# Split products of a two-block transformer: three 256-column matmuls per weight tile become a 512-column one and a 256-column one

## The chip, the core and the metric

The program runs on one core of a Trainium2 chip. The metric is the device time of one execution in microseconds. Lower is better. Operands and result are in device memory, and all work between them is timed.

## What is computed

Two residual blocks of depth 2 work on 256 tokens of width 1024. The first (A) has an adaptive modulation, a mix of dilated attention, a recurrent state scan and spatial gating, and a gated feed-forward net with a short convolution. The second (B) has two gated feed-forward nets around a mix of attention and a depthwise convolution, and a gated projection. Cut to the parts that carry the large products:

```python
def first_block(...):
    for l in range(DEPTH):
        h = modulate(rms_norm(x, norm_mix[l]), sh1, sc1)
        p = h @ w_in[l]
        ...
        branch = jnp.einsum('bsnw,nwd->bsnd', ys, w_branch[l])
        merged = jnp.sum(gates * branch, axis=2)
        x = x + gt1[:, None, :] * (merged @ w_out[l])
        h = modulate(rms_norm(x, norm_ffn[l]), sh2, sc2)
        x = x + gt2[:, None, :] * conv_gated_ffn(h, ffn_w_up[l], ...)

def conv_gated_ffn(h, w_up, conv_w, conv_b, w_down):
    up = h @ w_up
    ...
    return (jax.nn.gelu(a) * g) @ w_down
```

All operands are float32.

## The kernel before, in words

Activations lie with features on the partitions and the 256 tokens along the free dimension (S = 256). A large product runs over tiles of 128 output features by 128 input features, here called k-tiles. Since TensorE takes the operands in a rounded form (fp32r), each operand is cut in two: a rounded large part (`hi` of a weight, `h` of an activation) and the rest (`lo`, `l`). A k-tile is then three matmuls that add up in one PSUM bank (`mm3`, L163 to L166): hi with h, hi with l, lo with h, each with 256 columns. Each loads its 128x128 weights by itself.

Weights come from device memory in pieces of up to 1024 columns (`wload`, L122): a DMA to `raw` (L133, SyncE's queue), ScalarE rounds to `hi` (L137), VectorE subtracts to `lo` (L138). The buffers are rings (`ring`), so loads and splits run ahead of the matmuls by a few pieces. Activations are split by `split` (L194; ScalarE L201, VectorE L202).

`fpair` (L168) fills one bank of 512 columns with two output tiles. Four banks (tag `mm`) go round for this. The bank is then read by whatever the stage does with it: VectorE multiplies by a row of norm factors (L993 in `ffn_b`, L1189 and L1195 in `mix_b`), or merges (L867 and L868 in `branch`), or ScalarE applies a function. `down` (L927) fills half a bank with an output tile of 22 k-tiles. `tpair` (L182) is the product with tokens on the partitions.

The stages run one after the other: `mix_a`, `ffn_a` for each layer, then `ffn_b`, `mix_b`, `ffn_b`, `pe_b` for each layer. In the mixes, chains of dependent small steps (attention, state scan, convolution) are put between the large products in program order by `Order`. In `mix_b` the convolution's last 24 taps of 4 tiles run on VectorE (L1183), while TensorE computes gates. Within an engine, instructions run in program order, which the build has already rearranged: a split of weights stands ahead of the reads of earlier banks.

The lines around the change are these:

```python
        mm(ps, w[0], x[0], start=first, stop=False)
        mm(ps, w[0], x[1], start=False, stop=False)
        mm(ps, w[1], x[0], start=False, stop=last)
```

Of the kernel before, what the change touches and what calls it, by code (L numbers as in the profile page):

```python
# [17 lines left out]
S = 256  # L18
# [32 lines left out]
class K:  # L51
    def __init__(self, tc, ctx, ins):
# [4 lines left out]
        self.hp = E(tc.tile_pool(name="hp", bufs=17))  # L57
# [59 lines left out]
    def ring(self, kind):  # L117
        """The next slot of the weight buffers; further pools take part in turn."""
# [65 lines left out]
    def tpair(self, w, x, tt):  # L184
        ps = self.ps()
        mm = self.nc.tensor.matmul
        sl = slice(tt * 128, tt * 128 + 128)
        for k in range(8):
            h, l = w(k * 256, 256)
            mm(ps[:, :256], x[k][0][:, sl], h, start=k == 0, stop=False)  # L190
            mm(ps[:, :256], x[k][1][:, sl], h, start=False, stop=False)  # L191
            mm(ps[:, :256], x[k][0][:, sl], l, start=False, stop=k == 7)  # L192
# [38 lines left out]
    def rms(self, x, spread=True, tail=False, both=False):  # L231
        """1/rms of the tokens on all partitions: in PSUM, or in SBUF with spread; with both also tokens on partitions."""
# [22 lines left out]
    def headsum(self, sq, n, ps=None):  # L255
        """Sums of 64-row halves of the n [128, S] slices of sq, tokens on partitions: [128, n*2*2]."""
# [8 lines left out]
    def headback(self, r, i, ps):  # L265
        """Spreads column group i of r back over the rows of each half: [128, S] into ps."""
# [63 lines left out]
# ------------------------------------------------------------------ block A  # L330
# [11 lines left out]
class LayerA:  # L342
    """Per-layer columns and small weights of block A."""

    def __init__(self, G, l, pool, cact, first=None, late=None):
# [10 lines left out]
        else:  # L356
            # the columns of the first modulation before all else
# [26 lines left out]
def mod_cols(G, L, i, norm):  # L384
    """(A, shift) with h = x*rstd*A + shift."""
# [342 lines left out]
def mix_a(G, L, x, l, mp, pre, dbg=None):  # L728
# [841 lines left out]
```

## Time and profile before

| | |
|---|---|
| time, median of 3 runs | 2327.91 us (2326.52 to 2330.79) |
| span of the profiled execution | 2323.2 us |
| median less span | 4.7 us |
| busy TensorE matmul / weight load | 2240.6 / 2142.4 us |
| busy VectorE / ScalarE | 1677.5 / 1276.9 us |
| data moved | 416.69 MB, mean 179 GB/s |

The profiled execution has no time of its own beside its span, so the span is set against the median of the runs. Matmuls are pipelined and their ends are modelled, so TensorE's busy share says little of how fast it goes. What counts is the distance between the starts of two matmuls, or their number in a stretch.

### The profile page before, as it was taken

How to read it: one execution, taken by the hardware profiler on the slowest of the kernel's cores; microseconds unless marked ns; L12 is line 12 of the kernel's file. 1: busy time of each engine (PE TensorE's matmuls, PEld its weight loads, DVE VectorE, ACT ScalarE, POOL GpSimd, SP SyncE). 2: the span in 40 equal slices, each digit the busy share in tenths (PEclk: the TensorE clock that was granted, in tenths of full speed). 3: DMA queues.
4: the chain of work that ended last, by engine and by line, in shares of the span. 5: the costliest groups of instructions: out<-in, count | busy, mean ns of one | idle time of the engine just before them, and what ended most of it. 6: DMA issues, size and time to landing. Idle time of an engine off the chain costs nothing.

```text
span 2323.2 us, 46766 instructions
## 1 busy us (share of the span) xinstructions
PE 2240.6 (96%) x19122; PEld 2142.4 (92%) x19122; DVE 1677.5 (72%) x3026; ACT 1276.9 (55%) x2144; POOL 0.2 (0%) x4
## 2 busy tenths in 40 slices
PE   4999998978999999999999999999999999999999
PEld 4888898978888889999999999899999999999999
DVE  7777767757677776877576659976667655997665
ACT  4574545544457464565454457654455446666444
POOL 0000000000000000000000000000000000000000
PEclk9999999989999999999999999999999999999999
DMA  7634457777663445875576563466565556346653
GB/s 294 190 118 128 142 177 242 250 199 231 191 199 116 137 129 167 266 228 159 169 237 182 161 208 109 131 211 186 156 210 183 174 168 200 109 138 216 183 158 124
DMA packets 129117, 416.69 MB, mean 179 GB/s; under 512 B 14564, under 2 KB 20324, under 8 KB 128134
## 3 DMA queue, kind: packets, MB, share of 16 engines
q1 hardware_dynamic: 126718, 409.50, 55.8%
q10 hardware_dynamic: 2184, 4.19, 0.9%
q8 instruction: 150, 2.46, 0.4%
q14 instruction: 65, 0.53, 0.1%
HBM read 408.40 MB, written 5.24 MB: 178 GB/s over the span
## 4 chain that ended last, share of the span: by engine, by line
PE 80%; DMA 8%; DVE 7%; ACT 4%; issue 1%; SPq 0%; ACTq 0%; DVEq 0%
PE ps L164 23%; PE ps L165 22%; PE ps L166 22%; DMA raw<-in_ffn_up 3%; DVE lo L138 2%; DMA raw<-in_w_ada 2%; ACT hi L137 1%; DMA raw<-in_w_in 1%; PE rec L582 1%; PE rec L590 1%; DVE raw L369 1%; PE rec L1178 1%; DVE raw L338 1%; PE rec L636 1%; PE ps L191 1%
## 5 line engine op out<-in xcount | busy, mean ns | idle before, releaser
L164 PE MATMUL ps<-h,hi 128*128 128x256 f32 x5080 | 1438.4, 284 | 31.9 <-ACT h L201 29.6
L166 PE MATMUL ps<-h,lo 128*128 128x256 f32 x5080 | 1433.4, 283 | 14.7 <-DVE lo L138 14.7
L165 PE MATMUL ps<-l,hi 128*128 128x256 f32 x5080 | 1435.7, 283 | 4.9 <-DVE l L202 4.7
L137 ACT CAST hi<-raw 128x1024 fp32r<-128x1024 f32 (+1 forms) x724 | 704.7, 977 | 648.4 <-PE ps L165 377.8
L138 DVE TENSOR_TENSOR lo<-raw,hi 128x1024 fp32r<-128x1024 f32 (+1 forms) x724 | 818.9, 1133 | 301.6 <-ACT hi L137 299.0
L164 PEld LDWEIGHTS ps<-h,hi 128*128 128x128 f32 x5080 | 961.0, 190 | 47.2 <-ACT h L201 31.9
L166 PEld LDWEIGHTS ps<-h,lo 128*128 128x128 f32 x5080 | 962.3, 190 | 23.8 <-DVE lo L138 15.7
L165 PEld LDWEIGHTS ps<-l,hi 128*128 128x128 f32 x5080 | 961.8, 189 | 13.9 <-DVE l L202 6.8
L201 ACT CAST h<-t 128x256 fp32r<-128x256 f32 x172 | 68.6, 403 | 122.8 <-DVE t L996 96.1
L338 DVE SCALAR_TENSOR_TENSOR raw<-raw,cact 128x1024 f32<-128x1024 f32 x80 | 97.2, 1215 | 35.4 <-DMA raw<-in_w_ada 35.4
L202 DVE TENSOR_TENSOR l<-t,h 128x256 fp32r<-128x256 f32 x172 | 72.3, 423 | 60.5 <-ACT h L201 59.9
L993 DVE TENSOR_TENSOR t<-ps,r 128x512 f32<-128x512 f32 x88 | 60.8, 690 | 41.7 <-PE ps L166 41.3
L1183 DVE SCALAR_TENSOR_TENSOR cy<-cp,cwh,cy 128x256 f32<-128x256 f32 x192 | 85.0, 476 | 3.2 <-ACT cy L1181 2.9
L215 ACT ACTIVATE t<-x 128x256 f32<-128x256 f32 x96 | 38.5, 407 | 15.4 <-DVE x L964 8.5
L222 DVE TENSOR_TENSOR t<-t,t 128x256 f32<-128x256 f32 x87 | 36.4, 418 | 5.5 <-ACT t L215 4.3
L191 PE MATMUL ps<-hi,l 128*128 128x256 f32 x128 | 37.7, 294 | 0.0
L190 PE MATMUL ps<-hi,h 128*128 128x256 f32 x128 | 37.7, 294 | 0.0
L996 DVE TENSOR_TENSOR t<-t,t 128x256 f32<-128x256 f32 x88 | 36.8, 418 | 1.0 <-ACT t L995 1.0
L995 ACT ACTIVATE t<-t 128x256 f32<-128x256 f32 x88 | 36.2, 411 | 0.9
L192 PE MATMUL ps<-lo,h 128*128 128x256 f32 x128 | 36.7, 287 | 0.0
L960 ACT ACTIVATE t<-t 128x256 f32<-128x256 f32 x44 | 18.1, 415 | 29.0 <-DVE t L959 29.0
L416 ACT ACTIVATE t<-t,sh,am 128x256 f32<-128x256 f32 x32 | 18.1, 595 | 26.0 <-DVE am L395 22.5
(311 smaller groups left out, 1884.3 us busy)
## 6 DMA issues: line engine op xcount, KB each, us to landing
raw<-in_w_in SPq DMA_DIRECT2D x176, 512.0 KB, 4.2
raw<-in_ffn_in SPq DMA_DIRECT2D x176, 512.0 KB, 4.2
raw<-in_ffn_up SPq DMA_DIRECT2D x88, 512.0 KB, 5.4
raw<-in_w_ada SPq DMA_DIRECT2D x84, 512.0 KB, 4.8
raw<-in_ffn_out SPq DMA_DIRECT2D x64, 384.0 KB, 3.1
raw<-in_ffn_out SPq DMA_DIRECT2D x64, 320.0 KB, 3.2
raw<-in_w_branch SPq DMA_DIRECT2D x24, 512.0 KB, 4.1
raw<-in_ffn_down SPq DMA_DIRECT2D x32, 384.0 KB, 3.2
```

What stands on the lines that cost most here:

```text
L137: nc.scalar.copy(hi[:, :m], raw[:, :m])
L138: nc.vector.tensor_tensor(lo[:, :m], raw[:, :m], hi[:, :m], SUB)
L164: mm(ps, w[0], x[0], start=first, stop=False)
L165: mm(ps, w[0], x[1], start=False, stop=False)
L166: mm(ps, w[1], x[0], start=False, stop=last)
L191: mm(ps[:, :256], x[k][1][:, sl], h, start=False, stop=False)
L201: nc.scalar.copy(h, src)
L202: nc.vector.tensor_tensor(l, src, h, SUB)
L215: nc.scalar.square(sq, x[k])
L338: nc.vector.scalar_tensor_tensor(raw, raw, 1.0, cact, MUL, MUL, accum_out=mods[f // 8][:, f % 8:f % 8 + 1])
L993: nc.vector.tensor_tensor(v3(gu, 2), v3(ps, 2), rb, MUL)
L1183: stt(y, cp[:, jj:jj + S], cwh[:, jj * 4 + i:jj * 4 + i + 1], y, MUL, ADD)
```

## The change

An activation tile is now one tile [128, 2, 256] with the large part and the rest side by side. `mm3` sends both through the weight's large part in one matmul of 512 columns, into a whole bank; the weight's rest meets the activation's large part in a matmul of 256 columns, into the bank's first half. The two halves of the bank have then to be added: `fold` copies the second half out on ScalarE and adds the first on VectorE, `axpy` adds each half in a VectorE instruction. An output tile so takes a whole bank where two shared one. `tokens` takes the place of `tpair`, with 512-column weights as the moving operand.

```diff
     def mm3(self, ps, w, x, first, last):
         mm = self.nc.tensor.matmul
-        mm(ps, w[0], x[0], start=first, stop=False)
-        mm(ps, w[0], x[1], start=False, stop=False)
-        mm(ps, w[1], x[0], start=False, stop=last)
+        mm(ps, w[0], x.rearrange("p a b -> p (a b)"), start=first, stop=False)
+        mm(ps[:, :S], w[1], x[:, 0, :], start=False, stop=last)
...
+    def ftile(self, w, x, kt, c):
+        ps = self.ps()
+        for k in range(kt):
+            self.mm3(ps, w(c + k * 128), x[k], k == 0, k == kt - 1)
         return ps
+    def fpair(self, w, x, kt, cols):
+        return [self.ftile(w, x, kt, c) for c in cols]
+    def fold(self, ps, out=None):
+        t = self.tmp(S)
+        self.nc.scalar.copy(t, ps[:, S:])
+        out = t if out is None else out
+        self.nc.vector.tensor_tensor(out, ps[:, :S], t, ADD)
+        return out
+    def folds(self, pair, out=None):
+        out = self.tmp() if out is None else out
+        for i, ps in enumerate(pair):
+            self.fold(ps, out[:, i * S:(i + 1) * S])
+        return out
+    def axpy(self, o, ps, scale, x):
+        stt = self.nc.vector.scalar_tensor_tensor
+        stt(o, ps[:, :S], scale, x, MUL, ADD)
+        stt(o, ps[:, S:], scale, o, MUL, ADD)
...
-            ps = G.fpair(w, y, 4, ((dp % 2) * 1024, (dp % 2) * 1024 + 512))
+            ps = G.folds(G.fpair(w, y, 4, ((dp % 2) * 1024, (dp % 2) * 1024 + 512)))
...
-        ps = G.fpair(G.wload(w_in[f], 2048), xs, 8, (0, 1024))
-        gu = G.tmp()
-        nc.vector.tensor_tensor(v3(gu, 2), v3(ps, 2), rb, MUL)
-        sg = G.tmp(S)
-        nc.scalar.activation(sg, gu[:, :S], AF.Silu)
-        nc.vector.tensor_tensor(sg, sg, gu[:, S:], MUL)
+        gate, up = G.fpair(G.wload(w_in[f], 2048), xs, 8, (0, 1024))
+        sg = G.fold(gate)
+        tt(sg, sg, r, MUL)
+        nc.scalar.activation(sg, sg, AF.Silu)
+        tt(sg, sg, G.fold(up), MUL)
...
+    def evac(d, o, ps):
+        t = G.fold(ps)
+        tt(t, t, r, MUL)
+        nc.vector.scalar_tensor_tensor(o, t, 0.5, x[d], MUL, ADD)
+    return down(G, s, w_out, evac)
...
-        tt(v3(g, 2), v3(pair(7 + dp), 2), rb, MUL)
+        G.folds(pair(7 + dp), g)
+        tt(v3(g, 2), v3(g, 2), rb, MUL)
```

In `ffn_b` the factor r of the second half of the gate product moves to the end of the net, where `evac` now multiplies the output tile by it.

TensorE, in the second `ffn_b` of the last layer, at the start of an output tile (h and l are an activation's parts, hi and lo a weight's), before:

```order
L164 MATMUL ps_26731<-h_25945,hi_26721 128x256
L165 MATMUL ps_26731<-l_25946,hi_26721 128x256
L166 MATMUL ps_26731<-h_25945,lo_26722 128x256
L164 MATMUL ps_26731<-h_25949,hi_26721 128x256
L165 MATMUL ps_26731<-l_25950,hi_26721 128x256
L166 MATMUL ps_26731<-h_25949,lo_26722 128x256
```

and now (an h is now both parts side by side):

```order
L162 MATMUL ps_23272<-h_22614,hi_23262 128x512
L163 MATMUL ps_23272<-h_22614,lo_23263 128x256
L162 MATMUL ps_23272<-h_22617,hi_23262 128x512
L163 MATMUL ps_23272<-h_22617,lo_23263 128x256
L162 MATMUL ps_23272<-h_22620,hi_23262 128x512
L163 MATMUL ps_23272<-h_22620,lo_23263 128x256
```

Two k-tiles took six matmuls and six weight loads; three k-tiles now take six.

VectorE, in the first `mix_b`, from one gate on while the convolution's taps (cy) run, before:

```order
L1195 TENSOR_TENSOR gate_17331<-ps_17344,r_16630 128x512
L1111 TENSOR_TENSOR hv_17491<-aux_17409,r_16636 128x8
L1183 SCALAR_TENSOR_TENSOR cy_17208<-cp_16995,cwh_16632,cy_17208 128x256
L1112 TENSOR_SCALAR hv_17491<-hv_17491 128x8
L1183 SCALAR_TENSOR_TENSOR cy_17317<-cp_17101,cwh_16632,cy_17317 128x256
L138 TENSOR_TENSOR lo_17646<-raw_17643,hi_17645 128x1024
L138 TENSOR_TENSOR lo_17652<-raw_17649,hi_17651 128x1024
```

and now:

```order
L180 TENSOR_TENSOR gate_15229<-ps_15242,t_15276 128x256
L1200 SCALAR_TENSOR_TENSOR cy_15020<-cp_14836,cwh_14605,cy_15020 128x256
L1200 SCALAR_TENSOR_TENSOR cy_15115<-cp_14920,cwh_14605,cy_15115 128x256
L1200 SCALAR_TENSOR_TENSOR cy_15215<-cp_15017,cwh_14605,cy_15215 128x256
L1128 TENSOR_TENSOR hv_15371<-aux_15298,r_14609 128x8
L135 TENSOR_TENSOR lo_15419<-raw_15416,hi_15418 128x1024
L180 TENSOR_TENSOR gate_15229<-ps_15259,t_15279 128x256
L1129 TENSOR_SCALAR hv_15371<-hv_15371 128x8
L135 TENSOR_TENSOR lo_15425<-raw_15422,hi_15424 128x1024
L1214 TENSOR_TENSOR gate_15229<-gate_15229,r_14603 128x512
```

The multiplication by r stays (now from SBUF), and two additions of 256 columns (L180) stand ahead of it, each with a bank and a ScalarE copy behind it.

VectorE, in a `branch` of the first `mix_a`, one merged pair of tiles and its neighbours (uv, ST, W, Q, X, R belong to the state scan), before:

```order
L867 SCALAR_TENSOR_TENSOR gate_3321<-gate_3321,ps_3681 128x512
L628 TENSOR_SCALAR ST_3712<-rec_3709,Pe_2854 128x64
L868 TENSOR_TENSOR mg_2414<-mg_2414,gate_3321 128x512
L611 TENSOR_TENSOR W_3003<-rec_3718,W_3003 64x64
L611 TENSOR_TENSOR W_3003<-rec_3721,W_3003 64x64
L138 TENSOR_TENSOR lo_3850<-raw_3847,hi_3849 128x1024
```

and now:

```order
L180 TENSOR_TENSOR t_3260<-ps_3242,t_3261 128x256
L595 TENSOR_TENSOR X_3279<-AT_3052,ca 128x256
L595 TENSOR_TENSOR X_3363<-AT_3052,ca 128x256
L648 TENSOR_TENSOR ST_3225<-rec_3220,ST_3136 128x64
L135 TENSOR_TENSOR lo_3465<-raw_3462,hi_3464 128x1024
L649 TENSOR_SCALAR ST_3225<-ST_3225,Pe_2141 128x64
L180 TENSOR_TENSOR t_3260<-ps_3251,t_3264 128x256
L611 TENSOR_TENSOR Q_3272<-Q_3200,rec_3233 128x256
L882 SCALAR_TENSOR_TENSOR gate_2827<-gate_2827,t_3260 128x512
L629 TENSOR_TENSOR W_2267<-rec_3270,W_2267 64x64
L883 TENSOR_TENSOR mg_2092<-mg_2092,gate_2827 128x512
```

A merged pair now has two additions (L180) more on VectorE, and they wait for ScalarE's copies.

Over the program TensorE's 15,936 matmuls of 256 columns for large products (15,552 of `mm3`, 384 of `tpair`) become 5376 of 512 columns and 5184 of 256. VectorE has 692 more TENSOR_TENSOR of 128x256, 90 fewer of 128x512 and 48 more SCALAR_TENSOR_TENSOR of 128x256. ScalarE has 560 more copies of 128x256 and 10 fewer of 128x512.

## Rows read from the trace of the kernel before

**Rows 1.** The page: busy time (share) xinstructions, VectorE and granted clock in slices.

```profile
PE 2240.6 (96%) x19122; PEld 2142.4 (92%) x19122; DVE 1677.5 (72%) x3026; ACT 1276.9 (55%) x2144; POOL 0.2 (0%) x4
...
DVE  7777767757677776877576659976667655997665
...
PEclk9999999989999999999999999999999999999999
```

**Rows 2.** Longest waits of all engines: us in total, times, longest us.

```profile
ACT hi L137 <- PE ps L165: 377.8, 291, 6.9
...
PE ps L164 <- ACT h L201: 29.6, 9, 13.7
...
PE ps L166 <- DVE lo L138: 14.7, 5, 11.7
```

**Rows 3.** Timeline of PE, an output tile of `ffn_b`: start us, us.

```profile
1600.17 0.28 PE L164 MATMUL ps<-h,hi 128*128 128x256 f32 x1
...
1600.52 0.28 PE L164 MATMUL ps<-h,hi 128*128 128x256 f32 x1
```

**Rows 4.** Windows: first products of `ffn_b`, then `down`, then a stretch of `mix_a`.

```profile
1560.00:1660.00 100.00, 100.00 (x852) 100.00 (x850) 67.20 (x90) 47.26 (x71) 0.00 (x0) 1.00 0.56 171
...
1308.00:1364.00 56.00, 56.00 (x469) 56.00 (x468) 34.21 (x50) 28.65 (x43) 0.00 (x0) 1.00 0.68 207
...
54.20:61.70 7.50, 7.50 (x68) 7.50 (x67) 6.84 (x11) 5.01 (x7) 0.00 (x0) 1.00 0.65 194
```

**Rows 5.** Window: a stretch at half clock, large matmuls alone on PE (0.41 us each).

```profile
387.10:390.30 3.20, 3.20 (x17) 3.20 (x16) 2.92 (x5) 2.40 (x4) 0.00 (x0) 0.50 1.00 270
```

**Rows 6.** Timeline of PE: four matmuls of two columns, and the next one.

```profile
68.72 0.61 PE L262 MATMUL rec<-ca,t 128*128 128x2 f32 x4 [2.51 <-ACT t L478]
69.19 0.36 PE L166 MATMUL ps<-h,lo 128*128 128x256 f32 x1
```

**Rows 7.** Groups by line and form, whole program: busy us, mean ns.

```profile
L164 PE MATMUL ps<-h,hi 128*128 128x256 f32 x5080 | 1438.4, 284 | 31.9 <-ACT h L201 29.6 <-ACT hi L137 2.1
...
L164 PE MATMUL aux<-h,hi 128*128 128x256 f32 x72 | 21.0, 294 | 0.0
...
L164 PE MATMUL ps<-pj,hi 128*128 128x256 f32 x32 | 10.5, 329 | 0.0
```

**Rows 8.** The same view, VectorE and ScalarE.

```profile
L138 DVE TENSOR_TENSOR lo<-raw,hi 128x1024 fp32r<-128x1024 f32 x532 | 648.1, 1221 | 184.3 <-ACT hi L137 181.9 <-PE rec L638 0.7
...
L993 DVE TENSOR_TENSOR t<-ps,r 128x512 f32<-128x512 f32 x88 | 60.8, 690 | 41.7 <-PE ps L166 41.3
...
L961 DVE TENSOR_TENSOR t<-t,ps 128x256 f32<-128x256 f32 x40 | 16.5, 413 | 6.4 <-ACT t L960 6.4
L585 ACT COPY Y<-rec 128x256 f32<-128x256 f32 x40 | 14.8, 369 | 31.6 <-PE rec L582 31.5
...
L998 DVE SCALAR_TENSOR_TENSOR x<-ps,x 128x256 f32<-128x256 f32 x32 | 13.5, 422 | 1.2
...
L868 DVE TENSOR_TENSOR mg<-mg,gate 128x512 f32<-128x512 f32 x16 | 10.9, 683 | 0.1
L867 DVE SCALAR_TENSOR_TENSOR gate<-gate,ps 128x512 f32<-128x512 f32 x16 | 10.9, 683 | 8.4 <-PE ps L166 8.3
```

**Rows 9.** Windows: the gates beside the convolution in the two `mix_b`.

```profile
1400.00:1480.00 80.00, 79.90 (x612) 74.10 (x611) 78.58 (x186) 55.47 (x118) 0.00 (x0) 1.00 0.31 96
1972.00:2052.00 80.00, 79.89 (x614) 74.11 (x613) 78.57 (x186) 56.24 (x118) 0.00 (x0) 1.00 0.31 95
```

**Rows 10.** Windows: the start, the first `mix_a`, the first `ffn_a`.

```profile
0.00:75.00 75.00, 43.15 (x282) 38.38 (x283) 53.77 (x123) 37.67 (x64) 0.20 (x4) 0.98 0.77 277
75.00:367.00 292.00, 289.58 (x2787) 256.06 (x2786) 216.29 (x480) 159.77 (x291) 0.00 (x0) 1.00 0.47 150
388.00:617.00 229.00, 204.25 (x1638) 201.36 (x1637) 157.76 (x265) 110.44 (x176) 0.00 (x0) 0.93 0.74 227
```

In the windows of Rows 4, 5, 9 and 10 the columns are: the window, its length, busy us (xinstructions) of PE, PEld, DVE, ACT and POOL, the granted clock, the DMA share and GB/s.

More of the change, by code (lines that the diff above doesn't have):

```diff
@@ L182, in fmulti, with tokens @@
         return ps
-    def tpair(self, w, x, tt):
-        ps = self.ps()
+    def tokens(self, ws, x):
         mm = self.nc.tensor.matmul
-        sl = slice(tt * 128, tt * 128 + 128)
+        ps = [self.ps() for _ in range(2)]
         for k in range(8):
[L189 to L192, printed above, removed]
+            h, l = ws[k // 4](k % 4 * 512, 512)
+            for t, p in enumerate(ps):
+                xh, xl = (x[k][:, i, t * 128:t * 128 + 128] for i in range(2))
+                mm(p, xh, h, start=k == 0, stop=False)
+                mm(p, xh, l, start=False, stop=False)
+                mm(p, xl, h, start=False, stop=k == 7)
         return ps
@@ L429, in shifted @@
     for i, f in enumerate(ids):
-        p = halves(ps)[i]
+        p = G.fold(ps[i])
         nc.scalar.activation(z[:, i, :], p, AF.Copy, scale=L.omm[:, f:f + 1])
@@ L724, in attention_a @@
     yield 0.6
-    out[pair] = G.split(po[:, :S], pool=mp, tag="ys", bufs=9)
+    out[pair] = G.split(po[:, :S], pool=mp, tag="ys", bufs=4)
 def mix_a(G, L, x, l, mp, pre, dbg=None):
@@ L784, in start, with values @@
         O.add(f"r{p}", rwkv_pair(G, L, mp, p, zkr[p][:, 0, :], zkr[p][:, 1, :], zv[p], zwa, tw, sg, yr, O), 1.0)
-    def values(i):
-        w = G.wload(w_in[l, 4 + i], 2048)
-        for t in range(2):
-            ps = G.tpair(w, h, t)
-            nc.scalar.copy(V[t][:, i * 256:i * 256 + 256], ps[:, :256])
-            O.advance(cost / 2)
+    def values():
+        for t, ps in enumerate(G.tokens([G.wload(w_in[l, 4 + i], 2048) for i in range(2)], h)):
+            nc.scalar.copy(V[t], ps)
+            O.advance(cost)
     def heads(i):
@@ L799, in gmlp_v @@
         gv.extend(mp.tile([128, 512], F32, tag="V", name=G.nm("gv"), bufs=2) for _ in range(2))
-        for i in range(2):
-            w = G.wload(w_in[l, 15 + i], 2048)
-            for t in range(2):
-                ps = G.tpair(w, h, t)
-                act(gv[t][:, i * 256:i * 256 + 256], ps[:, :256], AF.Gelu_apprx_tanh)
-                O.advance(cost / 2)
+        for t, ps in enumerate(G.tokens([G.wload(w_in[l, 15 + i], 2048) for i in range(2)], h)):
+            act(gv[t], ps, AF.Gelu_apprx_tanh)
+            O.advance(cost)
     def gmlp_u(i):
         u = mp.tile([128, 2, S], F32, tag="qk", name=G.nm("gu"), bufs=2)
-        act(u, v3(pair(13 + i), 2), AF.Gelu_apprx_tanh)
+        act(u, v3(G.folds(pair(13 + i)), 2), AF.Gelu_apprx_tanh)
         gu.append(u)
@@ L852, in gates @@
             g = mp.tile([128, 512], F32, tag="gate", name=G.nm("gate"), bufs=4)
-            act(g, pair(17 + 4 * n + dp), AF.Tanh, scale=0.5)
+            G.folds(pair(17 + 4 * n + dp), g)
+            act(g, g, AF.Tanh, scale=0.5)
             out.append(g)
@@ L876, in mix_a @@
     z_kr(2)
-    values(0)
-    values(1)
+    values()
     z_v(1)
@@ L954, in ffn_a @@
         ps = first[f] if f < 2 else G.fpair(G.wload(G.ins["ffn_up"][l, f], 2048), h, 8, (0, 1024))
-        a, g = halves(ps)
+        a = G.fold(ps[0])
         t = G.tmp(S)
@@ L960, in ffn_a @@
         nc.scalar.activation(t, t, AF.Gelu_apprx_tanh)
-        nc.vector.tensor_tensor(t, t, g, MUL)
-        s.append(G.split(t, pool=mp, tag="s", bufs=46))
+        nc.vector.tensor_tensor(t, t, G.fold(ps[1]), MUL)
+        s.append(G.split(t, pool=mp, tag="s", bufs=23))
     gt = gate_cols(G, L, 1, 1.0)
-    return down(G, s, G.ins["ffn_down"][l], lambda d, o, ps: stt(o, ps, gt[:, d:d + 1], x[d], MUL, ADD))
+    return down(G, s, G.ins["ffn_down"][l], lambda d, o, ps: G.axpy(o, ps, gt[:, d:d + 1], x[d]))
 class LayerB:
@@ L1077, in attention_b @@
     yield 0.9
-    out[j] = G.split(po[:, :S], pool=mp, tag="ysb", bufs=16)
+    out[j] = G.split(po[:, :S], pool=mp, tag="ysb", bufs=7)
 def mix_b(G, L, x, l, mp, bias, dbg=None):
@@ L1154, in mix_b @@
         q = mp.tile([128, 2, S], F32, tag="q", name=G.nm("q"), bufs=3)
-        nc.scalar.copy(q.rearrange("p a b -> p (a b)"), pair(i))
+        G.folds(pair(i), q.rearrange("p a b -> p (a b)"))
         qs.append(q)
@@ L1188, in mix_b @@
         t = mp.tile([128, 512], F32, tag="cvg", name=G.nm("t"), bufs=1)
-        tt(v3(t, 2), v3(pair(3 + i), 2), rb, MUL)
+        G.folds(pair(3 + i), t)
+        tt(v3(t, 2), v3(t, 2), rb, MUL)
         O.add(f"c{i}", conv(i, t), 0.6)
@@ L1277, in project @@
         for i in range(2 * len(hs)):
-            ps = G.fpair(w, pp, 2, (i * 512, i * 512 + 256))
-            t = tile()
-            nc.scalar.copy(t, ps)
+            t = G.folds(G.fpair(w, pp, 2, (i * 512, i * 512 + 256)), tile())
             nc.scalar.dma_start(G.pj[l][2 * hs[0] + i], t)
```

71 lines of the change are left out of this document (28 added, 43 removed).

## The prediction

> **What bounds the kernel now.** I read the page first: TensorE is busy 96% of the span, VectorE 72%, ScalarE 55%, and the granted clock is full in nearly every slice [rows 1]. The waits say who waits for whom: ScalarE waits 377.8 us to round weights until TensorE frees a buffer, while TensorE's own longest waits are 29.6 and 14.7 us [rows 2]. So weights stand ready, and the pace of TensorE sets the time. The next view has to tell what that pace is, since the duration of a matmul (0.28 us) is longer than the distance of two starts (1600.17 to 1600.52 for three, 0.117 each) [rows 3]. A window counts it: 852 matmuls in 100 us. Each that overlaps an edge is counted too, so the distance is (100 + 0.28) / 852 = 0.1177 us in the first products, and (56 + 0.28) / 469 = 0.1200 us in `down` [rows 4].
>
> 256 columns at one column a cycle of 2.4 GHz would be 0.1067 us. That columns go one a cycle is seen where the granted clock is 0.50, its lower level of 1.2 GHz: there the distance is (3.20 + 0.41) / 17 = 0.212 us [rows 5], and 256 / 1.2 GHz is 0.2133. At full clock 0.011 us of each 0.1177 is something else. What it is decides this change, because the change leaves the columns as they are (768 a k-tile) and takes one matmul and one weight load of three away. Two rows speak. Four matmuls of two columns, each with a weight load, take 69.19 - 68.72 = 0.47 us, 0.1175 each [rows 6]: with nothing to stream, the loads alone make the same pace. And in one stretch of `mix_a` the same 256-column matmuls run at (7.5 + 0.28) / 68 = 0.114 us [rows 4], so the pace is no fixed price of a column. Both fit a chain of weight loads, in which the next load starts when a matmul starts and takes a little longer than its 256 columns.
>
> **The change, part by part.**
>
> *TensorE.* The 512 columns need 512 / 2.4 = 0.2133 us, longer than the load of 0.1175 under them. No row before shows this matmul. From below its price is 0.2133; from above it is two of today's, 0.2354. I take 0.217, since the row nearest in kind [rows 6] puts the excess on loads, which are hidden here. The 256-column matmul behind it has the next load under it, so it keeps 0.1177 (from below 0.1067). A k-tile then costs 0.335 us (0.320 to 0.353), where three matmuls cost 0.3531, or 0.3600 in `down`. The three groups of the first of the three matmuls have 5080, 72 and 32 members [rows 7], so there are 5184 k-tiles; 6 x 8 x 22 = 1056 are in `down`. That gives 4128 x 0.0181 = 74.7 and 1056 x 0.0250 = 26.4 us. `tokens` makes 192 x 0.217 = 41.7 of 384 x 0.1177 = 45.2, 3.5 less. Together -104.6 us.
>
> The Trainium skill, "TensorE: Matmul & The Clock Gate", section "Back-to-back issue gap", gives an isolated warm matmul N / 2.4 + 2.5 ns, 0.1092 us at 256 columns and 0.2158 at 512. The 256-column figure doesn't hold here, the row has 0.1177; by the rule a k-tile would cost an estimated 0.325 and the term would be some -157 us.
>
> *Reading the banks.* 560 folds cost ScalarE 560 x 0.369 (the copy of 256 columns from PSUM) = 207 us and VectorE 560 x 0.413 (an addition with one operand in PSUM) = 231 us [rows 8]. VectorE also has 48 second halves of `axpy` at 0.422 = 20 us, and in `ffn_b` 88 multiplications of 0.690 become 88 of 256 columns, with 32 more at the end of the net (about 0.413 each: -11 us). VectorE goes from 1677 to about 1917 us, ScalarE from 1277 to about 1480. Over a span of some 2260 that is 85% and 65%, so most of it hides beside TensorE. It costs nothing where the engine has room: in `ffn_b` VectorE is busy 67.2 of 100 us [rows 4], and 22 pairs with 0.57 more each over some 120 us bring it to about 80%. A bank now holds one tile of 8 k-tiles (2.7 us), and three others stand behind it, so a fold has 8 us before TensorE waits.
>
> *Where there is no room.* First, the gates of `mix_b` beside the convolution. There VectorE is busy 78.58 of 80 us [rows 9]. Ten pairs of tiles are read in that window, 20 folds x 0.413 = 8.3 us, 6.9 more than the 1.4 that are free. The stage grows by these, and the gain of its 160 k-tiles (2.9 us) is not had: 9.8 us for each `mix_b`, +19.6. Queued behind VectorE there are the next gates' folds, and behind them TensorE's banks.
>
> Second, the merges. A merged pair has 8 k-tiles, 2.68 us in future. VectorE's share is a split of weights, a multiplication and an addition, 1.221 + 0.683 + 0.683 = 2.59 us [rows 8], and two folds make it 3.41. 16 such pairs in `branch` and 8 in `mix_b` are 0.73 us over, 17.5 us if nothing had been split ahead. The ring holds a few splits and a merge has four pairs, so I take +10.
>
> Third, the ends of stages, where the next stage's first matmuls wait for the last tile: in four `ffn_b` a fold and a multiplication more (0.369 + 0.413 + 0.413 = 1.2), at six other ends one more `axpy` half (0.422), at the very end a fold (0.78). That is 8.1 us; partly beside the next splits, so +6.
>
> Fourth, what isn't gained because TensorE doesn't set the pace: in the first 75 us it is busy 43 [rows 10], 94 k-tiles, 1.7 us; in the first `ffn_a` it is busy 204 of 229 us at a granted clock of 0.93, waiting for transfers, and I drop a third of its 10 us. Together +5. The DMA queues carry the same bytes.
>
> The sum: -104.6 + 19.6 + 10 + 6 + 5 = -64 us. From the span of 2323.2 that is 2259.2; the runs' median is 4.7 above that span, so **2264 us**.
>
> **The rivals.**
>
> *The excess goes with the columns.* Then 512 columns cost two times 0.1177, TensorE gains nothing, and the tolls stay: 2 x 6.9 in `mix_b`, some 8 in the merges (0.59 over the old 2.82), 6 at the ends: +28, **2356 us**. For it: 0.1177 is steady through whole nets [rows 4]. Against it: the stretch at 0.114, and the loads of [rows 6]. The point from which it decides: tolls of 41 us are paid for once a k-tile costs 41 / 5184 = 0.0079 us less than today's mean of 0.3545, which is 0.3466, or 0.229 for the 512-column matmul; above that the kernel is slower.
>
> *VectorE holds the mixes.* In the first `mix_a` it is busy 216 of 292 us [rows 10]; 74 folds and 8 halves add 34, which makes 89% of a shortened stage, in program order, with the chain of the state scan between them. If every late fold stops the chain, both mixes keep their old time or more, and only the six nets gain: 6 x (352 x 0.0181 + 176 x 0.0250) = 64.6 us, less 14 (convolution), 14 (merges in full), 8 and 5: -24, **2304 us**. For it: VectorE's slices of 9 in [rows 1]. Against it: ScalarE's long waits for free weight buffers, which are room to be late.
>
> *The load vanishes wholly.* If the 256-column matmul too goes at its columns' time, 0.1067, because its own load is over long before, a k-tile costs 0.324: 4128 x 0.0291 + 1056 x 0.0360 + 3.5 = 161.6, less 41: **2207 us**. Against it: the load of the next weight still lies under just these columns. The page's rule above would come to about the same.
>
> **How the numbers follow.** The forecast has a chance of 0.5, with a range of its own of 2240 to 2290 (excess of the 512-column matmul 0 to 0.009 us, tolls 30 to 55). VectorE holding the mixes has 0.2, the load vanishing 0.15, the excess by column 0.15. The range from 2205 to 2330 takes in the first two and most of the third; it leaves the last out. This measurement tells 0.2%, 4.7 us, from no change. Faster than that are the first three, less the slow edge of the second: 0.80; within 0.2%: 0.06; slower: 0.14.
>
> **What would show it.** The starts of a 512-column matmul and the one behind it 0.217 us apart, and the next 0.118: right; 0.235: the first rival. About 10,700 large matmuls in place of 15,936. In a window of `ffn_b` VectorE near 80% and no wait of TensorE for L180. In `mix_b` beside the convolution VectorE without a gap over some 87 us, and TensorE waiting there for banks that VectorE or ScalarE frees. A granted clock that falls in the mixes would make the prediction wrong, as would TensorE waiting for folds in the nets.

## The result and the profile after

The changed kernel takes 2396.62 us (2391.57 to 2400.83, 4 runs), the kernel before 2327.59 us beside it: a ratio of 1.0303, 95% interval 1.0282 to 1.0323. It is 3.0% slower, where 2.7% faster was forecast.

The page of the changed kernel, with the busy line, VectorE's busy tenths and the granted clock, answers to [rows 1]:

```profile
PE 2259.9 (94%) x13746; PEld 1881.9 (78%) x13746; DVE 1869.8 (78%) x3676; ACT 1424.8 (59%) x2684; POOL 0.2 (0%) x4
...
DVE  7877868498688887788677669987778767998767
...
PEclk9999999899899999899999999999999999989999
```

TensorE has 5376 matmuls fewer and is busy about as long as before. VectorE is busy 192 us more and ScalarE 148 us more. The weight loads no longer fill TensorE's time (78%, before 92%). Whether that helps is a question of the pace. The timeline of TensorE in an output tile of the third net (start, us) answers to [rows 3]:

```profile
1659.78 0.39 PE L162 MATMUL ps<-h,hi 128*128 128x512 f32 x1
1660.01 0.28 PE L163 MATMUL ps<-h,lo 128*128 128x256 f32 x1
...
1660.84 0.39 PE L162 MATMUL ps<-h,hi 128*128 128x512 f32 x1
1661.07 0.28 PE L163 MATMUL ps<-h,lo 128*128 128x256 f32 x1
```

Three k-tiles take 1660.84 - 1659.78 = 1.06 us, 0.353 each, and a 512-column matmul takes 0.23 of it. Before, three 256-column matmuls took 0.353. The windows say the same (first products and `down` of this net, the convolution's stretch in both `mix_b`, a moment behind it, and the first `mix_a`; columns as in [rows 4, 9, 10]):

```profile
1640.00:1700.00 60.00, 60.00 (x342) 52.25 (x341) 46.03 (x75) 34.45 (x65) 0.00 (x0) 1.00 0.57 183
1735.00:1780.00 45.00, 45.00 (x257) 39.05 (x256) 30.75 (x47) 23.31 (x36) 0.00 (x0) 1.00 0.67 208
1445.20:1538.00 92.80, 87.47 (x486) 70.55 (x484) 87.80 (x211) 66.12 (x144) 0.00 (x0) 0.98 0.28 90
2030.60:2124.20 93.60, 88.24 (x486) 71.12 (x484) 87.83 (x211) 66.19 (x145) 0.00 (x0) 0.96 0.27 90
1559.00:1563.50 4.50, 4.50 (x21) 3.94 (x21) 4.30 (x9) 1.70 (x4) 0.00 (x0) 0.73 0.51 174
75.00:377.00 302.00, 293.64 (x2243) 225.25 (x2242) 234.17 (x541) 176.33 (x347) 0.00 (x0) 0.98 0.44 144
```

A k-tile costs 2 x (60 + 0.34) / 342 = 0.3529 us in first products (before 0.3531) and 2 x (45 + 0.34) / 257 = 0.3528 in `down` (before 0.3600). VectorE is busy 46 of 60 us there, 77%, so the nets are still TensorE's. In the first `mix_a` TensorE stood still for 8.4 us, before for 2.4 [rows 10].

The groups by line and form (busy us, mean ns, idle before), for [rows 7, 8]:

```profile
L162 PE MATMUL ps<-h,hi 128*128 128x512 f32 x5120 | 1853.9, 403 | 72.5 <-DVE h L224 43.6 <-ACT hi L134 13.8 <-DVE t L180 13.2
L163 PE MATMUL ps<-h,lo 128*128 128x256 f32 x5120 | 1460.4, 287 | 7.4 <-DVE lo L135 7.4
...
L178 ACT COPY t<-ps 128x256 f32<-128x256 f32 x564 | 201.3, 366 | 116.1 <-PE ps L163 115.1
L180 DVE TENSOR_TENSOR t<-ps,t 128x256 f32<-128x256 f32 x440 | 182.1, 419 | 24.5 <-ACT t L178 23.5
```

The folds cost what was put down for them: 366 and 419 ns, 0.369 and 0.413 forecast. TensorE's idle time ahead of the first matmul of a k-tile is 72.5 us, against 31.9 [rows 7]. TensorE's longest waits (in all, times, longest), for [rows 2]:

```profile
PE ps L162 <- DVE h L224: 43.6, 16, 15.3
PE ps L162 <- ACT hi L134: 13.8, 3, 11.2
PE ps L162 <- DVE t L180: 13.2, 3, 9.9
```

L224 is VectorE's half of an activation's split: the chains that feed a product are late. Of its 43.6 us, 15.3 lie at the start of the program, where the kernel before waited 13.7 [rows 2]. One place shows how. First TensorE at the end of the first `mix_b`'s convolution, then VectorE:

```profile
1551.25 0.28 PE L163 MATMUL ps<-h,lo 128*128 128x256 f32 x1
1557.59 0.77 PE L162 MATMUL ps<-h,hi 128*128 128x512 f32 x1 [6.06 <-DVE h L224]
...
1559.01 0.63 PE L162 MATMUL ps<-h,hi 128*128 128x512 f32 x1
1559.43 0.41 PE L163 MATMUL ps<-h,lo 128*128 128x256 f32 x1
1559.65 0.63 PE L162 MATMUL ps<-h,hi 128*128 128x512 f32 x1
```

```profile
1549.05 0.42 DVE L180 TENSOR_TENSOR t<-ps,t 128x256 f32<-128x256 f32 x1
1549.38 1.75 DVE L1238 RECIPROCAL crs<-crs 128x256 f32<-128x256 f32 x1
1551.04 0.36 DVE L180 TENSOR_TENSOR t<-ps,t 128x256 f32<-128x256 f32 x1
...
1553.50 1.22 DVE L135 TENSOR_TENSOR lo<-raw,hi 128x1024 fp32r<-128x1024 f32 x1
...
1557.02 0.76 DVE L224 TENSOR_TENSOR h<-cy,h 128x256 fp32r<-128x256 f32 x2
```

The norm of the convolution (L1238 to L1245), splits of weights and additions share VectorE; the products with the convolution's output wait 6.06 us for it. Behind the wait a pair takes 1559.65 - 1559.01 = 0.64 us in place of 0.353: the granted clock has fallen to its lower level, and the window above has a mean of 0.73. The span and the mean granted clock of the whole execution, after and then before:

```profile
core 0: 2399.0 us, clock 0.977
```

```profile
core 0: 2323.2 us, clock 0.988
```

From a stage to the next, by VectorE's last write of x in each (us):

| | mix_a, ffn_a | mix_a, ffn_a | ffn_b | mix_b | ffn_b, pe_b | ffn_b | mix_b | ffn_b, pe_b |
|---|---|---|---|---|---|---|---|---|
| before | 387.7, 229.3 | 355.2, 197.4 | 194.8 | 170.5 | 216.2 | 185.6 | 169.8 | 213.8 |
| after | 398.3, 238.7 | 370.5, 205.8 | 199.2 | 184.2 | 215.1 | 186.1 | 185.4 | 212.9 |
| no additions | 398.2, 235.5 | 365.6, 196.2 | 197.3 | 171.7 | 215.2 | 185.3 | 171.0 | 213.1 |
| old token product | 389.7, 233.8 | 359.6, 205.6 | 197.1 | 187.1 | 214.1 | 186.0 | 184.0 | 211.5 |
| grouped | 395.8, 229.1 | 374.0, 203.4 | 194.3 | 181.3 | 211.2 | 182.5 | 182.6 | 208.5 |

(The last three rows are experiments told below.) Three of the four nets of the second block neither gain nor lose, the first is 4.4 us longer. The rest of the loss lies in the mixes and in `ffn_a`. Each row is one profiled execution. Three of the kernels below have the same first block (the joint tile, and the two with the form in the second block's nets alone); it ends there at 1166.1, 1162.8 and 1159.4 us, so differences of a few us in that block say little.

### The profile page after: what moved, and what is told of

It is laid out like the page before. It is cut to its first block, busy times and chain, and to the rows that moved or that the text cites. A ratio compares the mean times of both kernels' runs of the same rounds, so it can differ in the third digit from the quotient of the medians.

```text
span 2399.0 us, 37166 instructions
## 1 busy us (share of the span) xinstructions
PE 2259.9 (94%) x13746; PEld 1881.9 (78%) x13746; DVE 1869.8 (78%) x3676; ACT 1424.8 (59%) x2684; POOL 0.2 (0%) x4
## 4 chain that ended last, share of the span: by engine, by line
PE 76%; DVE 10%; DMA 9%; ACT 4%; issue 1%; SPq 0%; DVEq 0%; ACTq 0%
PE ps L162 42%; PE ps L163 22%; DVE lo L135 3%; DMA raw<-in_w_in 2%; DMA skew<-ohb 2%; DMA raw<-in_w_ada 2%; DMA raw<-in_ffn_up 2%; ACT hi L134 1%; PE rec L1195 1%; PE rec L608 1%; DMA raw<-in_w_out 1%; DVE raw L360 1%; PE rec L600 1%; DVE cy L1200 1%; DVE t L180 1%
## 5 line engine op out<-in xcount | busy, mean ns | idle before, releaser
L162 PE MATMUL ps<-h,hi 128*128 128x512 f32 x5120 | 1853.9, 403 | 72.5 <-DVE h L224 43.6
L163 PE MATMUL ps<-h,lo 128*128 128x256 f32 x5120 | 1460.4, 287 | 7.4 <-DVE lo L135 7.4
L178 ACT COPY t<-ps 128x256 f32<-128x256 f32 x564 | 201.3, 366 | 116.1 <-PE ps L163 115.1
L180 DVE TENSOR_TENSOR t<-ps,t 128x256 f32<-128x256 f32 x440 | 182.1, 419 | 24.5 <-ACT t L178 23.5
L224 DVE TENSOR_TENSOR h<-t,h 128x256 fp32r<-128x256 f32 x172 | 70.8, 420 | 11.5 <-ACT h L223 9.1
L180 DVE TENSOR_TENSOR gate<-ps,t 128x256 f32<-128x256 f32 x80 | 33.4, 419 | 13.6 <-ACT t L178 13.0
L1006 ACT ACTIVATE t<-t 128x256 f32<-128x256 f32 x88 | 36.2, 412 | 12.5 <-DVE t L1005 12.4
L244 DVE TENSOR_TENSOR t<-t,t 128x256 f32<-128x256 f32 x87 | 36.6, 421 | 8.4 <-ACT t L237 5.9
L1005 DVE TENSOR_TENSOR t<-t,r 128x256 f32<-128x256 f32 x88 | 37.3, 425 | 4.5 <-ACT r L274 1.8
L1007 DVE TENSOR_TENSOR t<-t,t 128x256 f32<-128x256 f32 x88 | 37.3, 425 | 3.7 <-ACT t L1006 1.0
L973 DVE TENSOR_TENSOR t<-t,t 128x256 f32<-128x256 f32 x44 | 18.6, 422 | 25.4 <-ACT t L972 25.0
L969 ACT ACTIVATE t<-t,vec 128x256 f32<-128x256 f32 x44 | 26.3, 599 | 10.0 <-DVE t L180 10.0
```

Source lines behind the costliest of these rows:

```text
L162: mm(ps, w[0], x.rearrange("p a b -> p (a b)"), start=first, stop=False)
L163: mm(ps[:, :S], w[1], x[:, 0, :], start=False, stop=last)
L178: self.nc.scalar.copy(t, ps[:, S:])
L180: self.nc.vector.tensor_tensor(out, ps[:, :S], t, ADD)
L224: nc.vector.tensor_tensor(l, src, h, SUB)
L1005: tt(sg, sg, r, MUL)
```

## The experiments

Theory A: the 512-column matmul saves almost nothing, since the excess over its columns belongs to every matmul of this kind, and the additions' tolls are then unpaid. Theory B: it does save what was forecast, and tolls ate more than that. The runs below tell these apart, and then size the tolls one by one.

**The price of a matmul by itself.** The model is left out; series of 160 or 240 matmuls run in its place.

```python
for k in range(8):                      # 20 times
    mm(ps, w[:, q:q + 128], x[k % 4], start=k == 0, stop=k == 7)        # 512 columns
...
    mm(ps[:, :384], w[:, q:q + 128], x[k % 4][:, :384], ...)
    mm(ps[:, :256], w[:, q:q + 128], x[k % 4][:, :256], ...)
    mm(ps, w[:, 0:128], x[k % 4], ...)                                  # same weights
    mm(ps, wb[:, q:q + 128], xb[k % 4], ...)                            # bf16
```

> This kernel leaves the model out: it runs series of 160 to 240 matmuls with one operand form each, rounded float32 or bfloat16, with nothing else at work except in the last two series (VectorE additions; transfers). If the price goes with the columns of a rounded float32 operand, the distance of two starts is about 0.230 us at 512, 0.173 at 384 and 0.117 at 256 columns also when TensorE is alone, and bfloat16 tells whether it is the type (0.216 at 512). If work beside TensorE (the splits of VectorE and ScalarE, transfers) slows the 512 columns, they take about 0.217 alone and 0.23 in the last two series. If it is the chain of weight loads, 512 is 0.217 everywhere.

Windows in five of the series, the first of 512 columns, 384 columns, 256 columns, 512 columns with the same weights, and 256 columns in bf16, and the timeline of 35 bf16 matmuls of 512:

```profile
22.00:42.00 20.00, 20.00 (x90) 16.57 (x89) 19.50 (x31) 0.00 (x0) 0.00 (x0) 1.00 0.00 1
50.00:75.00 25.00, 25.00 (x146) 25.00 (x145) 3.94 (x33) 0.00 (x0) 0.00 (x0) 1.00 0.95 343
77.00:94.00 17.00, 17.00 (x144) 17.00 (x143) 3.31 (x23) 0.00 (x0) 0.00 (x0) 1.00 0.31 117
153.00:185.00 32.00, 32.00 (x143) 26.50 (x142) 3.00 (x18) 0.00 (x0) 0.00 (x0) 1.00 0.00 1
...
223.00:238.00 15.00, 15.00 (x140) 13.45 (x138) 2.96 (x18) 0.00 (x0) 0.00 (x0) 1.00 0.00 1
```

```profile
188.65 7.72 PE L1407 MATMUL ps<-xb,wb 128*128 128x512 bf16 x35
```

With the length of one matmul at the edge added, the distances are 25.33 / 146 = 0.1735, 17.28 / 144 = 0.1200 and 32.39 / 143 = 0.2265 us. The columns alone are 0.1600, 0.1067 and 0.2133: the excess is 0.0132 to 0.0135 at each of three widths. It is neither proportional to the columns (the first rival) nor hidden under them (the forecast). In the 512-column series weight loads take 26.50 of 32 us, so loads have room to spare, and the excess stays. The additions and transfers meant for the last two series ran earlier in the trace: the additions beside the first series, the transfers mostly beside the 384 columns (DMA share 0.95). With VectorE busy 19.50 of 20 us a 512-column matmul takes 20.39 / 90 = 0.2266 us, as it does without; with 64 rows and with other weights each time it is 0.226 to 0.228. Beside many transfers only 384 columns were measured. In bf16 it is 15.27 / 140 = 0.1091 and (7.72 - 0.38) / 34 = 0.2159: 0.0025 over the columns. So each matmul of the rounded float32 form costs some 13 ns beyond its columns here, and a k-tile with two in place of three could save one such excess, not the 18 and 25 ns of the forecast.

**Both widths in turn, alone.** As before without the model: 512 and 256 columns in turn as in the change, all 512 of a bank ahead of its 256, three of 256, and both widths in bf16.

```python
    mm(ps, hi, x[k % 4], start=k == 0, stop=False)
    mm(ps[:, :S], lo, x[k % 4][:, :S], start=False, stop=k == 7)
```

> This kernel leaves the model out: six series of matmuls of rounded float32, with nothing beside them, as the k-tiles of the change (512 and 256 columns in turn), the same with the eight of 512 ahead of the eight of 256, as the k-tiles before (three of 256), 256 alone, 512 with two weights in turn, and the first in bfloat16. If each matmul has a fixed price of 13.4 ns whatever stands beside it, a k-tile takes 0.347 us in turn and grouped and 0.360 as three. If taking widths in turn costs something of its own, it takes some 0.350 in turn and 0.347 or less grouped.

Windows of the series in turn, grouped, and of three:

```profile
20.00:67.00 47.00, 47.00 (x273) 41.08 (x272) 2.83 (x17) 0.00 (x0) 0.00 (x0) 1.00 0.00 1
...
70.00:122.00 52.00, 52.00 (x301) 45.85 (x300) 3.17 (x19) 0.00 (x0) 0.00 (x0) 1.00 0.00 1
126.00:180.00 54.00, 54.00 (x453) 54.00 (x452) 3.17 (x19) 0.00 (x0) 0.00 (x0) 1.00 0.00 1
```

A k-tile costs 2 x 47.34 / 273 = 0.347 in turn, 2 x 52.34 / 301 = 0.348 grouped and 3 x 54.28 / 453 = 0.3595 with three; in bf16 it costs 2 x 48.33 / 297 = 0.3255 in turn. So the form is worth 12 ns where the series of three pays its full excess. In the kernels it is worth less: before, three cost 0.3531 in first products (11 ns each over the columns), and after, the pair costs 0.3529 (16 ns each).

**Three matmuls of 256 in the changed kernel.** All of the change stays but the 512-column matmul of `mm3` (`tokens` keeps its own); the fold reads the bank's first half twice and takes the larger of two equal numbers, and `axpy` reads it twice too.

```diff
-        mm(ps, w[0], x.rearrange("p a b -> p (a b)"), start=first, stop=False)
+        mm(ps[:, :S], w[0], x[:, 0, :], start=first, stop=False)
+        mm(ps[:, :S], w[0], x[:, 1, :], start=False, stop=False)
         mm(ps[:, :S], w[1], x[:, 0, :], start=False, stop=last)
...
-        self.nc.vector.tensor_tensor(out, ps[:, :S], t, ADD)
+        self.nc.vector.tensor_tensor(out, ps[:, :S], t, MAX)
...
```

> The changed kernel with banks and folds as they are, but each k-tile as three matmuls of 256 columns again (the first half of a bank holds the whole sum; the fold copies and takes the larger of two equal numbers). If the 512-column matmul saves only its fixed part, some 3 ns of 0.235 us, this is 15 us slower than the change, about 2412 us. If the 512-column form saves nothing it is equal, about 2397. If it hurts, this is faster than 2390.

2402.34 us, ratio 1.0342 (1.0320 to 1.0364). Against the change's 1.0303 the 512-column matmul is worth 0.0039, some 9 us; the two intervals just overlap, and their bounds leave -1 to 19. Theory B, by which it would be worth 100, falls.

**No additions.** The fold copies the first half out on ScalarE, `axpy` adds the first half alone; the second half of every bank is left out.

```diff
-        t = self.tmp(S)
-        self.nc.scalar.copy(t, ps[:, S:])
-        out = t if out is None else out
-        self.nc.vector.tensor_tensor(out, ps[:, :S], t, ADD)
+        out = self.tmp(S) if out is None else out
+        self.nc.scalar.copy(out, ps[:, :S])
...
-        stt(o, ps[:, S:], scale, o, MUL, ADD)
```

> The changed kernel without VectorE's additions: a fold is one ScalarE copy of the bank's first half, an axpy has one instruction; the products of the activations' rest are left out of the sums. VectorE has some 250 us less work. If VectorE's additions are the toll, nearly all of the 85 us comes back: about 2315 to 2325 us. If the toll is the longer way from a bank to its reader (the ScalarE copy and its queue, one tile a bank), little comes back: 2370 or more.

2349.99 us, ratio 1.0115 (1.0093 to 1.0137): the additions on VectorE cost 0.0188, 44 us, between the two figures that were expected. Both `mix_b` come back to 171.7 and 171.0 us. The window of the convolution in the first one:

```profile
1425.80:1509.70 83.90, 83.77 (x488) 69.90 (x487) 81.73 (x192) 64.78 (x145) 0.00 (x0) 1.00 0.30 103
```

It is 83.9 us long, in the changed kernel 92.8, with VectorE busy all but 2.2 us. Most of the wait behind it stays:

```profile
1527.24 0.77 PE L162 MATMUL ps<-h,hi 128*128 128x512 f32 x1 [4.59 <-DVE h L221]
```

L221 is the same half of the split, so of the 6.06 us only 1.5 go with the additions.

**No copies.** VectorE copies the first half out; ScalarE's copy, and the hop to it, is left out with the second half.

```diff
-        t = self.tmp(S)
-        self.nc.scalar.copy(t, ps[:, S:])
-        out = t if out is None else out
-        self.nc.vector.tensor_tensor(out, ps[:, :S], t, ADD)
+        out = self.tmp(S) if out is None else out
+        self.nc.vector.tensor_copy(out, ps[:, :S])
```

> The changed kernel without ScalarE's copies: a fold is one VectorE copy of the bank's first half; the products of the activations' rest are left out of the sums, and VectorE has as many instructions as in the change. If VectorE's work is the toll, this stays above 2380 us. If the hop through ScalarE's queue is, it falls to about 2330.

2383.19 us, ratio 1.0257 (1.0235 to 1.0278): some 11 us, with intervals just apart. VectorE's copy takes 421 ns where the addition took 419, so its work is the same. The hop over ScalarE costs something, VectorE's additions four times as much. First products of a net in this run, where the two widths stand in turn as in the change:

```profile
1240.00:1300.00 60.00, 60.00 (x347) 52.55 (x346) 49.35 (x79) 31.25 (x44) 0.00 (x0) 1.00 0.64 212
```

A k-tile costs 2 x 60.34 / 347 = 0.3478 us here, not 0.3529.

**Grouped.** In the changed kernel all 512-column matmuls of an output tile stand ahead of its 256-column ones (in `down` by piece of weights).

```diff
         for k in range(kt):
-            self.mm3(ps, w(c + k * 128), x[k], k == 0, k == kt - 1)
+            mm(ps, w(c + k * 128)[0], x[k].rearrange("p a b -> p (a b)"), start=k == 0, stop=False)
+        for k in range(kt):
+            mm(ps[:, :S], w(c + k * 128)[1], x[k][:, 0, :], start=False, stop=k == kt - 1)
...
```

> The changed kernel with the eight (in down eleven) matmuls of 512 columns of a tile ahead of its matmuls of 256. If taking widths in turn is what makes a k-tile cost 0.3505 us, it costs 0.347 or less and the kernel is 18 us or more faster than the change, 2376 or below. If the order is no matter, it stays at 2394.

2367.94 us, ratio 1.0201 (1.0178 to 1.0224), 24 us better than the change. First products of the third net:

```profile
1640.00:1700.00 60.00, 60.00 (x351) 52.88 (x350) 45.48 (x77) 34.17 (x66) 0.00 (x0) 1.00 0.50 164
```

2 x 60.34 / 351 = 0.3438 a k-tile, against 0.3529 in turn. VectorE has as much to do in this stretch (45.48 us, in turn 46.03).

**The joint tile alone**, in the kernel before: both parts of an activation in one tile, three matmuls as ever.

```diff
-        h = pool.tile([128, S], F32R, tag=tag, name=self.nm("h"), **kw)
-        l = pool.tile([128, S], F32R, tag=tag, name=self.nm("l"), **kw)
+        hl = pool.tile([128, 2, S], F32R, tag=tag, name=self.nm("h"), **kw)
+        h, l = hl[:, 0, :], hl[:, 1, :]
```

> The kernel before with one edit: the two parts of an activation lie in one tile, so a matmul on the large part waits for both, and rings count pairs. If this coupling is what makes mix_a 10 to 15 us longer (which neither leaving out the additions nor the copies takes back), this is 20 us or more slower than before. If not, it is as before, 2324.

2320.68 us, ratio 0.9982 (0.9968 to 0.9997): no toll.

**The old product with tokens on the partitions** in the changed kernel.

```diff
-        for t, ps in enumerate(G.tokens([G.wload(w_in[l, 4 + i], 2048) for i in range(2)], h)):
-            nc.scalar.copy(V[t], ps)
-            O.advance(cost)
+        for i in range(2):
+            w = G.wload(w_in[l, 4 + i], 2048)
+            for t in range(2):
+                ps = G.tpair(w, h, t)
+                nc.scalar.copy(V[t][:, i * 256:i * 256 + 256], ps[:, :256])
+                O.advance(cost / 2)
```

> The changed kernel with the products with tokens on the partitions in their old form (tpair, 256 columns, four readings a product). If the new form tokens lengthens mix_a, some 20 us come back (2375). If not, it stays at 2394 or is up to 7 us slower.

2374.67 us, ratio 1.0224 (1.0202 to 1.0245): `tokens` costs 18 us, and the stages say where: both `mix_a`, by 8.6 and 10.9 us. `tokens` issues its 48 matmuls in one piece before a step of a chain can come between, `tpair` 24 of half the width; that the chains are late for this reason was argued from the code, not tried.

**Both of these together.**

> The changed kernel with the 512-column matmuls of an output tile ahead of its 256-column ones (24 us gained alone) and the old product with the tokens on the partitions (18 us gained alone). If the two are separate terms: 2394 - 24 - 18 = 2352 us, ratio about 1.012, still slower, since the additions on VectorE (44) and the copies (11) stay and TensorE's saving is small. If both only remove the same stalls in the first mixes, about 2368, no better than grouping alone. If the cause were something else that both expose, the sum could pass the kernel before: under 2325.

2371.16 us, ratio 1.0200 (1.0178 to 1.0221), no better than grouping alone: the two gains are not separate terms. The first `mix_a` takes 396.6 us again, as in the grouped kernel (395.8), where the old product alone had 389.7. Which chain sets it there is not settled.

**Grouping without the form**: the kernel before, three matmuls of 256, the weights' large parts of a tile ahead of their rests.

```diff
             for k in range(kt):
-                self.mm3(ps[:, i * S:(i + 1) * S], w(c + k * 128), x[k], k == 0, k == kt - 1)
+                for j in range(2):
+                    self.nc.tensor.matmul(o, w(c + k * 128)[0], x[k][j], start=k + j == 0, stop=False)
+            for k in range(kt):
+                self.nc.tensor.matmul(o, w(c + k * 128)[1], x[k][0], start=False, stop=k == kt - 1)
...
```

> The kernel before (three 256-column matmuls a k-tile, no additions, no 512), with only the order changed: for each output tile first the weights' large parts with both parts of the activation, then the weights' rests with the activation's large part. If what grouping gained (24 us) came from the order alone (the weights' rest, made by VectorE, is needed later, so TensorE waits less), this gains too: some 5 to 20 us, ratio 0.992 to 0.998, and TensorE's waits for VectorE's rests shrink. If it came from the pace of 512-column matmuls standing next to each other, here nothing changes: ratio 0.998 to 1.002 with starts 118 ns apart as before.

2325.38 us, ratio 1.0001 (0.9989 to 1.0012). That the weights' rests are needed later is worth nothing in the kernel before; as far as this run tells, what grouping gained goes with the two widths.

**The form where VectorE has room**: the kernel before with the joint tile, and only the four nets of the second block in the new form, grouped.

```diff
...
+        gate, up = (G.ftile(w, xs, 8, c) for c in (0, 1024))
+        sg = G.fold(gate)
+        nc.vector.tensor_tensor(sg, sg, r, MUL)
+        nc.scalar.activation(sg, sg, AF.Silu)
+        nc.vector.tensor_tensor(sg, sg, G.fold(up), MUL)
...
```

> The kernel before with both parts in one tile, and only the four nets of the second block (up and down products) in the new form, 512-column matmuls of a tile ahead of its 256-column ones. All else is as before. If the price of the form is what the patterns showed (about 229 + 114 us/1000 a k-tile against 353 to 360) and VectorE has room in these nets, the stages gain what they gained in the grouped kernel, 5.0, 3.1 and 5.3 us for two nets and a projection, one net, and two nets and a projection, with the first net about 0.5: some 12 us of 2325, ratio 0.994 to 0.996. If the form gains nothing wherever it stands, ratio 0.998 to 1.001; if the additions cost also here, over 1.002.

2302.88 us (2299.49 to 2305.36), ratio 0.9905 (0.9887 to 0.9923): faster than both kernels, and more than the 12 us expected. Some 4 of the 22 us are the joint tile's. First products and `down` of the first net:

```profile
1185.00:1285.00 100.00, 100.00 (x583) 88.12 (x583) 79.83 (x131) 59.03 (x111) 0.00 (x0) 1.00 0.61 197
1300.00:1350.00 50.00, 50.00 (x290) 44.12 (x289) 33.28 (x53) 26.25 (x40) 0.00 (x0) 1.00 0.64 207
```

A k-tile costs 2 x 100.34 / 583 = 0.3442 and 2 x 50.34 / 290 = 0.3472, 8.9 and 12.8 ns less than before: 1408 x 0.0089 + 704 x 0.0128 = 21.5 us over the four nets, less their tolls. The second block is 17 us shorter in the trace (1133.6 us, before 1150.7); 4.5 of them lie in the two `mix_b`, which have not the form.

**The same in turn**, as in the change.

> The kernel before with only the four nets of the second block in the new form, as in the run that gained 22 us there, but with the 512-column and the 256-column matmuls in turn, as in the change. If the pace of the pair decides (232 + 118 in turn, 229 + 117 or 227 + 120 grouped), a k-tile loses 3 to 4 ns of what it gained, over 4 x 352 = 1408 k-tiles 4 to 6 us: some 2307 us, ratio 0.992 to 0.994. If in these nets the change as made gains nothing at all, as its own stages there said (215.1, 186.1 and 212.9 against 216.2, 185.6 and 213.8), ratio 0.997 to 1.000. If the order is of no account, 0.9905 as grouped.

2309.51 us, ratio 0.9941 (0.9926 to 0.9956). The expectation counted 1408 k-tiles and forgot those of `down`; with 2112 the loss by order is 6 to 8 us. The ratios differ by 0.0036, 8 us, with intervals just apart. The windows of the same places:

```profile
1185.00:1285.00 100.00, 100.00 (x568) 87.05 (x568) 76.87 (x126) 57.23 (x108) 0.00 (x0) 1.00 0.57 187
1300.00:1350.00 50.00, 50.00 (x291) 44.10 (x290) 34.85 (x54) 26.33 (x41) 0.00 (x0) 1.00 0.66 207
```

0.3533 in first products, no gain at all, as in the change; 0.3460 in `down`, where the grouped run has 0.3472 and the change, in turn too, 0.3528. So the pace in turn is not one figure, and the order tells only in first products. The second block is 7.2 us shorter than before; the first, which has only the joint tile, is 10.2 us shorter in this execution, though the joint tile alone was worth 4.

## Why the prediction was wrong

**The step that failed first** is "I take 0.217, since the row nearest in kind [rows 6] puts the excess on loads, which are hidden here". A 512-column matmul took 0.2265 in a series of its own with loads hidden, and the pair 0.353 in this kernel. The row was also misread: 0.1175 is a mean, and in the trace the first of the four distances is 0.133 us and the others 0.111 to 0.112. That is below the 0.114 to 0.120 of the 256-column matmuls, so these loads were faster than the pace they were to explain. Of the -104.6 us, the -101.1 of the k-tiles came out at 4128 x 0.0002 + 1056 x 0.0072 = 8.4 us gained by the windows, and 9 us by the run with three of 256. By itself this puts some 93 us between forecast and result. The warning was written down as the first rival, with the point from which it decides: above 0.229 for the 512-column matmul the kernel is slower. At 0.353 less the 0.118 kept for the second matmul, the row read 0.235. The rival's mechanism was wrong too (the excess is per matmul, the same at three widths), but its price held in this stream, and of its 2356 us the tolls were too small.

**The tolls** were forecast at 41 us; from the 69 us lost and the 9 gained they are some 78. Additions (44), `tokens` (18) and copies (11) come near this when taken one at a time, but gains of this kind did not add up in the run with two of them.
- The additions in `mix_b` were right as a cost. The convolution's window was to grow by 6.9 us and grew from 83.3 to 92.8 and 93.6; it holds 20 additions as counted, 8.4 us. VectorE wasn't gapless there (87.8 of 92.8 busy), and TensorE didn't wait for banks: its longest waits there are for a weight's rest and for a tap of the convolution, which VectorE does late. Not foreseen was what comes behind it: the stall of 6.06 us before the last products, most of which stays without additions. The two stages lost 13.7 and 15.6 us, where 6.9 each were to be lost in the window, and all but 1.2 each came back without additions. TensorE's waits in the window, and the same stretch in the kernel before, from the first to the last of the convolution's taps on VectorE:

```profile
PE ps L163 <- DVE lo L135: 1.9, 1, 1.9
PE rec L1225 <- DVE cy L1200: 1.8, 1, 1.8
```

```profile
1399.10:1482.40 83.30, 82.00 (x626) 75.62 (x624) 81.81 (x191) 58.09 (x121) 0.00 (x0) 1.00 0.33 100
```

- `tokens` was booked as a gain of 3.5 us and cost 18 when measured alone.
- The merges (+10) were not tried apart. Both `mix_a` lost 25.9 us with them in; without additions 20.9 of that stays, with the old token product 6.4.
- The first block's nets were to gain and lost 9.4 and 8.4 us. The longest waits for folds (9.9 us for L180) and for rounded weights (11.2 us) are in the first. In the second, without additions, the loss is gone (196.2 us); how the first's divides was not tried.
- The ends: forecast +6, not tried apart. The joint tile has no term in the forecast, and cost nothing when it was tried alone.
- The clock was named as what would make the prediction wrong, but not priced: 1 - 0.977 over 2399.0 us at half speed gives an estimate of 110 us at the lower level, before 56. Part of that is idle time, so it doesn't add to the stalls in full.

**VectorE holding the mixes**, the rival with 2304 us, was right for the mixes: they take longer than before, all four. It was wrong in what it left to the nets, 64.6 us, by the same price of 0.335.

**What held**: the number of large matmuls (10,560, "about 10,700" in the prediction), the cost of a fold, VectorE near 80% in the nets (77%) and no steady wait for L180 there.

**Open**: why the excess of a matmul is 11 ns in one stream of the kernel, 13 in another and 16 with the widths in turn, when alone the widths in turn show 13 to 14; why grouping gains 9 ns a pair in first products and nothing in `down` or alone, and why the pace in turn is 0.3478 in one run and 0.3529 in another. Which chain makes `mix_a` longer was not found either.

## What to carry to other kernels

Before a matmul is made wider to save issues, run a series of each width by itself: what is left when the columns are taken off tells whether there is anything to save, and one that sets the whole sum should not be taken from a row of another kind. A saving on the engine that bounds most of a program is spent only where the other engines have room: the same form, grouped, loses 2.0% everywhere, and gains 1.0% in the second block's nets alone; in turn it loses 3.0% and gains 0.6%. Some 0.2% of each gain is the joint tile's. Price a stall by the stretch at the lower clock behind it as well, not by the wait alone.

## What the hardware showed that was not expected

- In a steady series a rounded-float32 matmul starts 13.2 to 13.5 ns later than its columns alone would have it, at 256, 384 and 512 columns; in bf16 it is 2.5 ns (0.1091 and 0.2159 us). The Trainium skill, "TensorE: Matmul & The Clock Gate", section "Back-to-back issue gap", gives N / 2.4 + 2.5 ns for an isolated warm matmul: the trace's series agrees for bf16, and not for the rounded form, where the measurement decides.
- The order of two widths in one bank can matter in a kernel: first products took 0.3529 us a pair in turn and 0.3438 grouped, while alone both take 0.347 to 0.348. In `down` it did not (0.3460 in turn, 0.3472 grouped, in the runs with the form in the nets alone).
- Behind a stall of 6.06 us TensorE went on at its lower level of 1.2 GHz (a pair in 0.64 us, its columns alone in 768 / 1.2 GHz); the window behind the stall has a mean granted clock of 0.73.
